# Hybrid attention and convolution layer: two transfers moved to ScalarE's queue, fewer warm-up matmuls, and a new order of work from changed planning constants

## Chip, cores and metric

The kernel runs on one core of a Trainium2 chip. The metric is the device time of one execution in microseconds (us); the median of several runs counts. A profile is one execution recorded by the hardware profiler.

## The reference, cut to what matters

```python
h = rmsnorm(x, norm_g)                      # x: 1024 x 1024 float32
proj = h @ w_in                             # w_in: 1024 x 5632
q, k, v, a_gate, c_val, c_glu, c_gate = split(proj)
# 16 query heads, 4 key/value heads of 64; softmax over three dilated causal windows
y_att = attention_branch(q, k, v, a_gate)   # (window, dilation): (128,1) (512,4) (2048,16)
# depthwise causal convolution of 31 taps over c_val * sigmoid(c_glu), layer norm, silu, gate
y_conv = conv_branch(c_val, c_glu, c_gate, ...)
x = x + concat(y_att, y_conv) @ w_out       # w_out: 2048 x 1024
out = rmsnorm(x, final_norm_g)
```

## The kernel before

All large products run on TensorE (PE) in a split form: a float32 operand is stored as a rounded high part and the remainder (hhi and hlo for the normalised input, wh and wl for the weights), and a product is three matmuls, high by high, low by high and high by low. ScalarE (ACT) makes the high part by a cast (line 250), VectorE (DVE) or a DMA that adds (line 298, on GpSimd's queue, POOL) the remainder.

The phases follow one another and overlap. In the **opening** (`prepare(0)`, lines 556 to 603) the eight blocks x0 to x7 of 128 rows are loaded, their mean squares taken (x0 by ACT, x1 by DVE, the others by ACT), the rows scaled by DVE (line 590) with the gain that PE has spread over the partitions (`gbc`, line 568), transposed by PE (`xT`), and split. Meanwhile PE runs `WARM` dummy transposes into a bank called `idle` (line 548), and `MORE` further ones after the first blocks (line 596). `parameters()` loads the taps and norm parameters into `rows` and has PE transpose them (`par_ps`, line 610). In the **body** PE computes 44 column blocks of the projection (`ps`), scores and outputs of 8 pairs of heads, while DVE convolves; which piece is issued in which section is in `SECTIONS`. In the **passage** to the end, the layer norm of the convolved channels (`layer_norm`, tiles cc, lst, rb) meets the first half of the product with w_out (`att_part`: ya is loaded, split into yha and yla, and multiplied by woah and woal into opsa). In the **last phase** (`conv_part`) yc is loaded and split for eight blocks of 128 rows, multiplied into opsc, added to z, normalised and stored.

No order of instructions is written by hand. Every operation goes into a list (`Plan.op`) with an engine and a cost. `Plan.order` (lines 304 to 421) simulates the engines with these costs and with limits on how many buffers of a group are live (`LIMITS`), and picks for each engine the operation that can start first, by priority among those that are ready. A priority is the position in the list less a boost; `TUNE` holds the boosts of the kinds of work. The order so found is fixed for each engine, SP (which issues most DMAs) and POOL included. So a constant of the simulated costs changes the order of all engines. A DMA is simulated here:

```python
if e in ("SP", "POOL"):
    dma = max(dma, t + 1.1) + self.dma_time[i]
    done = dma + 0.9
```

`dma_time` is the size by 300 GB/s for SP and by 175 GB/s otherwise. `after=` in `load` adds a dependency for the plan alone: `ya` is planned after the last woal (line 1034).

Of the kernel before, what the change touches and what calls it, by code (L numbers as in the profile page):

```python
# [16 lines left out]
P = 128  # L17
# [14 lines left out]

LIMITS = {"x": 5, "raw": 1, "raw_oc": 1, "raw_oa": 2, "wh": 3, "wl": 3, "tab": 2, "e": 7, "pt": 4, "vs": 4, "vc":
          4, "turn": 2, "opsa": 2, "score": 2, "hc": 5, "c": 7, "t": 1, "g": 1, "gl": 7, "y": 2, "ag": 4, "cc": 5,
          "qs": 5, "qf": 4, "kdh": 9, "kdl": 6, "yc": 2, "ya": 2, "zc": 7, "za": 3}

RESERVE = {"e": 7, "pt": 3}
BANKS = {"mm": 3, "sc": 2, "tp": 2, "o": 1}  # L40
WARM = 55
LATE = C_CG + 6 * P
MORE = (10, 12)
TUNE = {"w": 195, "use": 240, "ln": 65, "att": 240, "conv": 5, "wo": 215, "woa": -20, "ap": 0, "wait": 0.2116}
SECTIONS = [("k0 q0 h1 v", 0), ("h2 a0 q1", 1), ("h3 a1 q2 a2", 1), ("q3 h4", 1), ("h5 k1 a3 q4", 1), ("h6 a4 q5",
            1), ("c0 h7 a5 q6", 1), ("c1 q7 a6 a7 c2 c3", 1), ("c4 c5", 1), ("c6 c7", 0)]


def score_tables():
# [105 lines left out]
def ap_of(v):  # L155
    return v.ap() if isinstance(v, View) else v
# [5 lines left out]
class Plan:  # L162
# [5 lines left out]
    def __init__(self, tc, slots, limits):  # L168
        self.tc, self.nc = tc, tc.nc
        self.slots = slots  # L170
        self.limits = limits
        self.ops = []
        self.hold = []
        self.moved = []
        self.prio, self.boost = [], 0
        self.ranks = {}
        self.tables = {}
# [115 lines left out]
    def load(self, out, src, after=None):  # L293

        self.op("SP", 0.48, lambda: self.nc.sync.dma_start(out.ap(), ap_of(src)), [out], [src, after])

    def add_into(self, dst, x):
        self.op("POOL", 1.0, lambda: self.nc.gpsimd.dma_start(ap_of(dst), x.ap(), accum_op=ALU.add), [dst], [x, dst])  # L298

# [4 lines left out]
    def order(self):  # L304
        ops = self.ops
        n = len(ops)
        users, need = [[] for _ in ops], [0] * n
        for i, (_, _, _, deps, _) in enumerate(ops):
            need[i] = len(deps)
            for d in deps:  # L310
                users[d].append(i)
        left = {}
        for _, _, _, _, bufs in ops:
            for b in bufs:
                left[b] = b.left
        free = {k: [(0.0, j) for j in range(v[2])] for k, v in self.slots.items()}
        held, inuse, taken, bank = set(), {}, {}, {}
        clock = {e: 0.0 for e in ("PE", "ACT", "DVE", "SP", "POOL")}
        ready = {e: [] for e in clock}
        at = [0.0] * n  # L320
        self.when = at[:]
        for i in range(n):
            if not need[i]:
                ready[ops[i][0]].append(i)
        dma, table = 0.0, None
        out = []
        reserving = [i for i, op in enumerate(ops) if any(b.group in RESERVE for b in op[4])]
        first, last = reserving[0], reserving[-1]

        done_ops, oldest = [False] * n, 0  # L330

        def start_of(i):
            if i > oldest + self.ahead:
                return None
            t = max(at[i], clock[ops[i][0]])
            want, groups = {}, {}
            for b in ops[i][4]:
                if not b.fixed and b not in held:
                    want[b.kind] = want.get(b.kind, 0) + 1
                    if b.group:  # L340
                        groups.setdefault(b.group, []).append(b.rank)
            for k, c in groups.items():
                if inuse.get(k, 0) + len(c) > self.limits[k] or max(c) != taken.get(k, 0) + len(c) - 1:
                    return None
            for b in ops[i][4]:
                if b in bank and bank[b][0] != ops[i][0]:
                    t = max(t, bank[b][1])
            for k, c in want.items():
                keep = 0
                if k == "c4" and i > oldest + 16:  # L350
                    if first - self.near < oldest <= last and not any(g in RESERVE for g in groups):
                        keep = sum(max(n - inuse.get(g, 0), 0) for g, n in RESERVE.items())
                    if i > oldest + self.near:
                        keep += self.spare
                if len(free[k]) < c + keep:
                    return None
                t = max(t, sorted(free[k])[c - 1][0])
            return t

        while len(out) < n:  # L360
            best = None
            for e, todo in ready.items():
                now, pick = None, None
                for i in sorted(todo, key=self.prio.__getitem__):
                    t = start_of(i)
                    if t is None:
                        continue
                    soon = t - TUNE["wait"] if self.prio[i] < i - 300 else t
                    if now is None or soon < now - 1e-9:
                        now, pick, start = soon, i, t  # L370
                        if soon <= clock[e]:
                            break
                if pick is not None and (best is None or start < best[0]):
                    best = (start, pick)
            if best is None:
                raise RuntimeError(f"no slots: {oldest}, {inuse}, { {k: len(f) for k, f in free.items()} }, "
                                   f"{[(i, [b.name for b in ops[i][4]]) for r in ready.values() for i in sorted(r)[:3]]}")
            t, i = best
            e, cost, _, _, bufs = ops[i]
            if i in self.tables and self.tables[i] != table:  # L380
                table = self.tables[i]
                cost += 1.3
            ready[e].remove(i)
            for b in bufs:
                if not b.fixed and b not in held:
                    held.add(b)
                    if b.group:
                        inuse[b.group] = inuse.get(b.group, 0) + 1
                        taken[b.group] = taken.get(b.group, 0) + 1
                    b.slot = min(free[b.kind])[1]  # L390
                    free[b.kind].remove(min(free[b.kind]))
            end = t + cost
            clock[e] = end
            done = end + self.LATENCY
            if e in ("SP", "POOL"):
                dma = max(dma, t + 1.1) + self.dma_time[i]
                done = dma + 0.9
            elif e == "DVE":
                done = end + 0.13
            for b in bufs:  # L400
                if b.kind in PSUM_KINDS:
                    bank[b] = (e, done)
            same = {"PE": end, "ACT": end + 0.03}.get(e, done)
            for u in users[i]:
                at[u] = max(at[u], same if ops[u][0] == e else done)
                need[u] -= 1
                if not need[u]:
                    ready[ops[u][0]].append(u)
            for b in bufs:
                left[b] -= 1  # L410
                if not left[b] and not b.fixed:
                    free[b.kind].append((done, b.slot))
                    if b.group:
                        inuse[b.group] -= 1
            self.when[i] = t
            out.append(i)
            done_ops[i] = True
            while oldest < n and done_ops[oldest]:
                oldest += 1
        self.clock = clock  # L420
        return out

    def trace(self):
# [1 line left out]
        last = {}  # L425
        self.dma_time = {}
        for i, (e, _, _, _, bufs) in enumerate(self.ops):
            if e in ("SP", "POOL"):
                self.dma_time[i] = 4.0 * self.moved[i] / (300e3 if e == "SP" else 175e3)
        for i in self.order():  # L430
            engine, _, fn, _, bufs = self.ops[i]
# [32 lines left out]
def layer_kernel(tc, x, norm_g, w_in, conv_w, conv_b, ln_g, ln_b, w_out, fin_g, tab, out):  # L464
# [91 lines left out]
    def prepare(half):  # L556
        xs = []
        for j in range(4):
            tb = 4 * half + j
            xs.append(c4([P, D], f"x{tb}"))  # L560
            pl.load(xs[j], x[tb * P:(tb + 1) * P, :])
            if tb == 1:
                pl.load(gain, norm_g.rearrange("(o d) -> o d", o=1))
            if tb in first_w:
                raw[tb] = load_raw(first_w[tb])
# [494 lines left out]
    def conv_part(tb):  # L1060
# [18 lines left out]
        if final:  # L1079
            pl.tt(z[:, 0:512], z[:, 0:512], fin[:, 0:512], ALU.mult)  # L1080
            pl.act(z[:, 0:512], z[:, 0:512], AF.Copy, scale=r)
            pl.store(out[rows, 0:512], z[:, 0:512])
            pl.stt(z[:, 512:D], z[:, 512:D], r, fin[:, 512:D], ALU.mult, ALU.mult)
            pl.store(out[rows, 512:D], z[:, 512:D])
        else:
# [79 lines left out]
```

## Time and profile before

| what | us |
|---|---|
| median of three runs | 899.86 |
| lowest and highest run | 898.11, 900.07 |
| the profiled execution's own time | 898.14 |
| its span, first to last instruction | 896.3 |
| PE busy in the span | 873.2 |
| DVE busy | 655.8 |
| ACT busy | 592.8 |
| POOL busy | 53.3 |

The span is what the trace covers; the execution's own time has 1.8 us more around it. PE busy is the time with at least one matmul under way, dummies included. In the rows below, times are us from the start of the span; `<-` in brackets names what ended an idle time; SPq is SP's queue of DMA issues and PEld PE's loading of weights. PEclk is the granted TensorE clock as a share of full speed.

### The profile page before, as it was taken

What the parts mean: (1) busy time and instruction counts of PE and PEld (TensorE: products, weight loads), DVE (VectorE), ACT (ScalarE), POOL (GpSimd) and SP (SyncE); (2) the same over time, 40 slices, a digit from 0 to 9 for tenths busy, and PEclk for the clock granted to TensorE, in tenths of its full rate; (3) what the DMA queues carried; (4) which work ended last, traced back from release to release, by engine and by line L of the source; (5) the groups of instructions that cost most, each with busy time, mean ns of one, the idle gap of its engine ahead of it and who ended that gap; (6) DMA issues with size and microseconds to landing.
All of it is one profiled execution on the core that took longest, in us unless ns stands there. A gap on an engine that the chain in (4) does not pass through costs nothing.

```text
span 896.3 us, 13046 instructions
## 1 busy us (share of the span) xinstructions
PE 873.2 (97%) x4493; PEld 720.2 (80%) x4493; DVE 655.8 (73%) x1506; ACT 592.8 (66%) x1392; POOL 53.3 (6%) x69
## 2 busy tenths in 40 slices
PE   8999999999999999999999999999999799999996
PEld 7888888888888788887887887888787678878885
DVE  5769996689699689789989779943649895625333
ACT  4777368677958867977977947983896744414111
POOL 0001001010010010010010110101000000000000
PEclk9999999999999999999999999999999799999999
DMA  7533607254553474545355744455773697777111
GB/s 266 164 71 58 153 3 165 50 116 77 138 111 81 100 150 108 139 71 143 78 112 143 165 94 130 89 137 112 217 261 141 204 363 238 252 217 229 71 48 47
DMA packets 104953, 123.53 MB, mean 138 GB/s; under 512 B 17941, under 2 KB 78357, under 8 KB 104888
## 3 DMA queue, kind: packets, MB, share of 16 engines
q1 hardware_dynamic: 97000, 94.40, 34.3%
q0 software_dynamic: 7888, 28.32, 17.9%
q8 instruction: 35, 0.57, 0.3%
q14 instruction: 30, 0.25, 0.1%
HBM read 65.35 MB, written 24.84 MB: 101 GB/s over the span
## 4 chain that ended last, share of the span: by engine, by line
PE 86%; DMA 7%; DVE 3%; ACT 2%; issue 1%; SPq 1%; POOL 0%; DVEq 0%; ACTq 0%; POOLq 0%
PE ps L237 52%; PE opsc L237 10%; PE opsa L237 7%; PE sc_near L237 3%; PE on L237 3%; PE of L237 3%; PE sc_far L237 2%; DMA y<-comb 2%; PE tp_p L235 1%; PE tp_m L235 1%; DMA rows<-in_ln_b 1%; PE tp_s L235 1%; DMA raw_oc<-in_w_out 1%; ACT e L252 1%; DMA yc<-yc_dram 1%; DMA x<-in_x 1%
## 5 line engine op out<-in xcount | busy, mean ns | idle before, releaser
L237 PE MATMUL ps<-hhi,wh 128*128 128x512 f32 (+1 forms) x720 | 288.1, 401 | 0.3 <-ACT hhi L250 0.2
L237 PE MATMUL ps<-hlo,wh 128*128 128x512 f32 (+1 forms) x720 | 279.6, 390 | 0.3 <-DVE hlo L265 0.3
L237 PE MATMUL ps<-hhi,wl 128*128 128x512 f32 (+1 forms) x720 | 188.7, 395 | 0.0
L237 PEld LDWEIGHTS ps<-hhi,wh 128*128 128x128 f32 x720 | 135.6, 188 | 31.4 <-issue 0.5
L237 PEld LDWEIGHTS ps<-hlo,wh 128*128 128x128 f32 x720 | 135.8, 189 | 27.6 <-DVE hlo L265 0.8
L237 PEld LDWEIGHTS ps<-hhi,wl 128*128 128x128 f32 x720 | 129.3, 188 | 27.9
L252 ACT ACTIVATE e<-e,near 128x256 f32<-128x256 f32 (+1 forms) x256 | 115.6, 488 | 22.2 <-DVE near L265 12.3
L269 DVE SCALAR_TENSOR_TENSOR c<-hc,taps,c 128x511 f32<-128x511 f32 (+14 forms) x120 | 88.4, 737 | 0.3
L269 DVE SCALAR_TENSOR_TENSOR c<-t,taps,c 128x511 f32<-128x511 f32 (+14 forms) x120 | 88.6, 738 | 0.0
L269 DVE SCALAR_TENSOR_TENSOR t<-hc,taps,t 128x511 f32<-128x511 f32 (+6 forms) x112 | 82.5, 736 | 0.8 <-ACT t L252 0.8
L237 PE MATMUL opsc<-woc,yhc 128*128 128x512 f32 (+1 forms) x272 | 80.8, 381 | 0.0
L252 ACT ACTIVATE e<-e,far 128x224 f32<-128x224 f32 (+1 forms) x128 | 54.0, 424 | 36.0 <-DVE far L284 35.7
L298 POOL DMA_DIRECT2D wl<-raw x40 | 34.7, 868 | 452.1 <-ACT wl L252 350.1
L237 PEld LDWEIGHTS opsc<-woc,yhc 128*128 128x128 f32 x272 | 50.2, 188 | 10.6
L252 ACT ACTIVATE fjunk<-zc 128x512 bf16<-128x512 f32 (+1 forms) x17 | 10.3, 606 | 68.0 <-DVE zc L265 67.8
L237 PE MATMUL opsc<-woc,ylc 128*128 128x512 f32 (+1 forms) x136 | 52.0, 382 | 1.5 <-DVE ylc L265 1.5
L284 DVE CUSTOM_DVE_ANT_0 e<-sc_near,tab 128x256 f32<-128x256 f32 (+1 forms) x128 | 45.0, 404 | 9.9 <-PE sc_near L237 9.2
L250 ACT CAST wh<-raw 128x1024 fp32r<-128x1024 f32 x44 | 46.0, 1044 | 1.6 <-DMA raw<-in_w_in 1.4
L237 PE MATMUL opsa<-woah,yla 128*128 128x512 f32 x112 | 45.5, 406 | 1.5 <-DVE yla L265 1.5
L237 PE MATMUL opsa<-woah,yha 128*128 128x512 f32 x112 | 45.4, 405 | 0.0
L237 PE MATMUL opsa<-woal,yha 128*128 128x512 f32 x112 | 45.0, 402 | 0.0
L252 ACT ACTIVATE e<-e,f 128x96 f32<-128x96 f32 (+1 forms) x128 | 44.5, 439 | 0.2 <-DMA f<-back 0.2
(166 smaller groups left out, 1405.1 us busy)
## 6 DMA issues: line engine op xcount, KB each, us to landing
raw<-in_w_in SPq DMA_DIRECT2D x44, 512.0 KB, 4.5
wl<-raw POOLq DMA_DIRECT2D x40, 512.0 KB, 4.9
x<-in_x SPq DMA_DIRECT2D x8, 512.0 KB, 8.5
tab<-in_tab SPq DMA_DIRECT2D x8, 512.0 KB, 3.4
c_dram<-c SPq DMA_DIRECT2D x8, 512.0 KB, 3.3
g_dram<-g SPq DMA_DIRECT2D x8, 512.0 KB, 2.8
raw_oa<-in_w_out SPq DMA_DIRECT2D x8, 512.0 KB, 5.7
raw_oc<-in_w_out SPq DMA_DIRECT2D x8, 512.0 KB, 7.4
```

Of the source, the lines that this page charges most:

```text
L235: nc.tensor.transpose(out.ap(), a.ap(), b.ap())
L237: nc.tensor.matmul(out.ap(), a.ap(), b.ap(), start=start, stop=stop)
L250: nc.scalar.copy(out.ap(), x.ap())
L252: nc.scalar.activation(out.ap(), x.ap(), func, **{k: ap_of(v) for k, v in kw.items()})
L269: lambda: self.nc.vector.scalar_tensor_tensor(out.ap(), a.ap(), ap_of(s), b.ap(), op0, op1),
L284: lambda: self.nc.vector.tensor_tensor_reduce(out.ap(), a.ap(), b.ap(), 1.0, ap_of(first), ALU.add, ALU.min, least.ap()),
L298: self.op("POOL", 1.0, lambda: self.nc.gpsimd.dma_start(ap_of(dst), x.ap(), accum_op=ALU.add), [dst], [x, dst])
```

## The change

x1 is loaded by ACT's queue, and the first half of the last output block is stored by it. The dummies go from 55 to 26, those after the first two blocks from 10 and 12 to 8 and 8. The plan assumes that a DMA lands 1.9 us after its bytes have moved instead of 0.9, counts the two DMAs on ACT as DMAs (at the rate of those not on SP), and gets other limits, boosts and sections.

```diff
-LIMITS = {"x": 5, "raw": 1, "raw_oc": 1, "raw_oa": 2, "wh": 3, "wl": 3, "tab": 2, "e": 7, "pt": 4, "vs": 4, "vc":
-          4, "turn": 2, "opsa": 2, "score": 2, "hc": 5, "c": 7, "t": 1, "g": 1, "gl": 7, "y": 2, "ag": 4, "cc": 5,
-          "qs": 5, "qf": 4, "kdh": 9, "kdl": 6, "yc": 2, "ya": 2, "zc": 7, "za": 3}
+LIMITS = {"x": 5, "raw": 1, "raw_oc": 1, "raw_oa": 2, "wh": 4, "wl": 3, "tab": 1, "e": 7, "pt": 4, "vs": 4, "vc":
+          4, "turn": 2, "opsa": 2, "score": 2, "hc": 7, "c": 7, "t": 1, "g": 1, "gl": 7, "y": 2, "ag": 4, "cc": 4,
+          "qs": 6, "qf": 4, "kdh": 9, "kdl": 5, "yc": 1, "ya": 2, "zc": 8, "za": 3}
-WARM = 55
+WARM = 26
-MORE = (10, 12)
-TUNE = {"w": 195, "use": 240, "ln": 65, "att": 240, "conv": 5, "wo": 215, "woa": -20, "ap": 0, "wait": 0.2116}
-SECTIONS = [("k0 q0 h1 v", 0), ("h2 a0 q1", 1), ("h3 a1 q2 a2", 1), ("q3 h4", 1), ("h5 k1 a3 q4", 1), ("h6 a4 q5",
-            1), ("c0 h7 a5 q6", 1), ("c1 q7 a6 a7 c2 c3", 1), ("c4 c5", 1), ("c6 c7", 0)]
+MORE = (8, 8)
+TUNE = {"w": 215, "use": 120, "ln": 65, "att": 240, "conv": -105, "wo": 155, "woa": -240, "ap": 20, "wait": 0.2116}
+SECTIONS = [("k0 q0 h1 v", 0), ("h2 a0 q1", 1), ("h3 a1 q2", 1), ("a2 q3 h4", 1), ("h5 k1 a3 q4", 1), ("h6 a4 q5",
+            1), ("c0 h7 a5 q6", 1), ("a6 c1 a7 q7 c2", 1), ("c5 c4 c3", 1), ("c6 c7", 0)]
...
+        self.sent = set()
...
+    def load_act(self, out, src):
+        self.op("ACT", 0.1, lambda: self.nc.scalar.dma_start(out.ap(), ap_of(src)), [out], [src])
+        self.sent.add(len(self.ops) - 1)
+
+    def store_act(self, dst, x):
+        self.op("ACT", 0.1, lambda: self.nc.scalar.dma_start(ap_of(dst), x.ap()), [dst], [x])
+        self.sent.add(len(self.ops) - 1)
...
-            if e in ("SP", "POOL"):
+            if e in ("SP", "POOL") or i in self.sent:
                 dma = max(dma, t + 1.1) + self.dma_time[i]
-                done = dma + 0.9
+                done = dma + 1.9
...
-            same = {"PE": end, "ACT": end + 0.03}.get(e, done)
+            same = done if i in self.sent else {"PE": end, "ACT": end + 0.03}.get(e, done)
...
-            if e in ("SP", "POOL"):
+            if e in ("SP", "POOL") or i in self.sent:
                 self.dma_time[i] = 4.0 * self.moved[i] / (300e3 if e == "SP" else 175e3)
...
-            pl.load(xs[j], x[tb * P:(tb + 1) * P, :])
+            (pl.load_act if tb == 1 else pl.load)(xs[j], x[tb * P:(tb + 1) * P, :])
...
-            pl.store(out[rows, 0:512], z[:, 0:512])
+            pl.store_act(out[rows, 0:512], z[:, 0:512])
```

## Rows read from the trace of the kernel before

**Rows 1.** Windows: stretch, length, PE, PEld, DVE, ACT, POOL busy (instructions), PEclk, DMA share, GB/s.
```profile
0.00:25.00 25.00, 20.71 (x142) 18.24 (x142) 13.82 (x30) 12.93 (x23) 1.02 (x8) 0.95 0.78 260
...
675.00:704.00 29.00, 22.86 (x99) 16.87 (x97) 26.82 (x43) 20.44 (x29) 0.00 (x0) 0.91 0.58 195
...
850.00:897.00 47.00, 38.92 (x191) 32.37 (x190) 14.15 (x35) 7.62 (x23) 0.00 (x0) 0.96 0.12 49
sum 897.00, PE 873.23 PEld 720.16 DVE 655.78 ACT 592.75 POOL 53.26; mean PE 45.96 PEld 37.90 DVE 34.51 ACT 31.20 POOL 2.80
```

**Rows 2.** Windows of PE alone in the passage: length, PE busy, PEclk, DMA share, GB/s.
```profile
700.00:705.00 5.00, 3.60 (x12) 0.50 1.08 347
705.00:710.00 5.00, 5.00 (x16) 0.63 0.67 211
```

**Rows 3.** Timeline of the opening: start, us, engine, line, operation, [idle before <-releaser].
```profile
0.74 1.28 ACT L252 ACT_TABLE_LOAD   x1 [0.74 <-PEq L1157]
0.74 0.87 SPq L295 DMA_DIRECT2D x<-in_x  x2
...
1.45 8.23 PE L235 MATMUL idle<-ident 128*128 128x128 f32 x55 [1.45 <-POOL ident masks.py:199]
...
4.49 1.06 ACT L252 ACTIVATE junk<-x 128x1024 bf16<-128x1024 f32 x1 [2.25 <-DMA x<-in_x]
...
5.81 1.23 DVE L290 CUSTOM_DVE_ANT_0 junk<-x 128x1024 bf16<-128x1024 f32 x1 [3.96 <-DMA x<-in_x]
...
9.61 1.98 PE L237 MATMUL gbc<-gain,avg 1*128 1x512 f32 x4
...
10.77 2.92 DVE L269 SCALAR_TENSOR_TENSOR x<-x,xst,gbc 128x512 f32<-128x512 f32 x4 [2.42 <-PE gbc L237]
...
21.54 0.66 PE L235 MATMUL par_ps<-ident,rows 34*128 34x34 f32 x8 [1.70 <-DMA rows<-in_ln_b]
```

**Rows 4.** PE's groups, 0 to 6 us, then 6 to 9 us: busy us, mean ns.
```profile
L235 PE MATMUL idle<-ident 128*128 128x128 f32 x23 | 4.7, 398 | 1.5 <-POOL ident masks.py:199 1.5
L235 PE MATMUL idle<-ident 128*128 128x128 f32 x30 | 3.4, 272 | 0.0
```

**Rows 5.** Windows of PE alone in the opening, the row from 3 to 4 us.
```profile
3.00:4.00 1.00, 1.00 (x6) 1.00 0.94 373
```

**Rows 6.** The tail: SP's timeline, then the stores of the tensor `out_dram`.
```profile
892.30 0.81 SPq L301 DMA_DIRECT2D out_dram<-zc  x2
...
L301 SPq DMA_DIRECT2D out_dram<-zc x9: 332/333/383, 815.9 to 892.7; - x9
```

**Rows 7.** DMA issues of the whole kernel: count, KB each, median us to landing.
```profile
raw<-in_w_in SPq DMA_DIRECT2D x44, 512.0 KB, 4.5
...
tab<-in_tab SPq DMA_DIRECT2D x8, 512.0 KB, 3.4
...
raw_oc<-in_w_out SPq DMA_DIRECT2D x8, 512.0 KB, 7.4
...
ya<-y_dram SPq DMA_DIRECT2D x8, 448.0 KB, 7.9
```

**Rows 8.** Timelines in the passage (SP, PE, ACT), and the tile woal.
```profile
696.07 0.39 SPq L295 DMA_DIRECT2D ya<-y_dram  x1
...
700.48 2.05 PE L237 MATMUL rb<-ident,lst 128*128 128x128 f32 x8 [4.28 <-DVE lst L269]
...
701.00 0.94 ACT L250 CAST yha<-ya 128x896 fp32r<-128x896 f32 x1 [0.22 <-DMA ya<-y_dram]
...
L265 DVE TENSOR_TENSOR woal<-raw_oa,woah x8: 1209/1216/1221, 643.5 to 696.3; 128x1024 fp32r<-128x1024 f32 x8
```

**Rows 9.** Last phase: the chain that ended last, and the tile yc.
```profile
799.90 89.04 PE opsc L237 x406
...
L250 ACT CAST yhc<-yc x8: 1032/1050/1054, 796.5 to 826.2; 128x1024 fp32r<-128x1024 f32 x8
L265 DVE TENSOR_TENSOR ylc<-yc,yhc x8: 1214/1219/1226, 798.6 to 829.2; 128x1024 fp32r<-128x1024 f32 x8
...
DMA to landing us min/median/max: 5.9/7.1/10.8
```

## The prediction

> **What bounds the kernel now.** I read the table of busy time by stretch first. PE is busy 873.23 us of a span of 896.3, so the bound is PE's own work plus 23.1 us in which it stands [rows 1]. Those stand in three places. In the first 25 us PE is idle 4.3 us; in the last row it is idle 8.1 us, of which 0.7 lie beyond the span, so 7.4 us; what is left, 23.1 - 4.3 - 7.4 = 11.4 us, is in the body. Of this, 6.1 us stand in one stretch, 675 to 704 us [rows 1], where the last projections end and the products with w_out begin. The reader is to see there also a granted clock of 0.91. The finer rows give its price: PE is busy 3.60 us at clock 0.50, then 5.00 us at 0.63 [rows 2]. At half level, 3.60 us does 1.8 us of work. A mean of 0.63 over 5 us is 3.7 us at the lower level (1.2 GHz) and 1.3 at the upper (2.4 GHz), which loses another 1.85. So this passage costs 6.1 + 1.8 + 1.9 = 9.8 us. Elsewhere the stalls are short, and DVE, ACT and DMA matter only through them. Thus there are three places to look at: the opening, the passage, and the tail after the last matmul.
>
> **Opening: fewer dummies.** The timeline of the opening shows PE on 55 dummies from 1.45 to 9.68, then the gain broadcast (gbc) at 9.61. DVE, which has the statistics of x0 and x1 finished earlier, stands 2.42 us until gbc comes, and normalises at 10.77 [rows 3]. With 26 dummies: 23 of them start before 6.0 us, and the later ones are faster, at a mean of 272 ns (pipelined) against 398 [rows 4]. The remaining 32 start in the 3.6 us to 9.6, 0.11 us each, so the 26th starts near 6.3 and PE is free at about 6.5. gbc then comes 3.1 us sooner, at 6.5; its first bank served DVE 1.16 us after its start (10.77 - 9.61), so would at 7.7. DVE's idle time began at 10.77 - 2.42 = 8.35, hence gbc is no longer last and the whole 2.42 us come off this step.
>
> What is late next? PE's transposes of the parameters (par_ps) wait 1.70 us for a landing of `rows<-in_ln_b` and start at 21.54 [rows 3]. PE takes its instructions in order. If par_ps keeps its place ahead of the transposes of x2, PE merely waits there 2.4 us longer and nothing is gained. If the new plan puts it behind them, the 2.4 us stay. The plan now assumes all loads 1.0 us later, both x2 and the parameter rows, so neither order is favoured. I take half, -1.2. Ends: -2.4, and +1.25 if less PE activity keeps the clock low for as long again as now (granted 0.95 over 25 us withholds 1.25 us of full-speed time [rows 1]). The cuts of MORE from 10 and 12 to 8 and 8 remove six fast dummies, 0.7 us that fit in PE's wait for DVE; I cost them at nothing. If that cover is gone they are worth 0.7, inside these ends.
>
> **Opening: x1 by ACT.** SP issues x0 and x1 in 0.87 us [rows 3], so gain, raw and x2 are issued about 0.43 us sooner. ACT issues x1 at 0.74 instead of some 1.18, if the issue stands before its table load. Behind the load of 1.28 us it would go out at 2.02, 0.84 us later [rows 3]. Behind this instruction on ACT stand only the table load and the warm-up; ACT then stands until x0 lands at 4.49, so they delay nobody. Would x1 land sooner? x0 is there at 4.49, x1 at 5.81, 1.32 us apart. From 3 to 4 us the 16 DMA engines are already at a share of 0.94 and move 373 GB/s [rows 5]: no room is left for a second stream. The Trainium skill (DMA: Bandwidth & Descriptors, Issuing engines are not separate DMA queues) says that transfers issued by the scalar, sync or gpsimd engine run on the same 16 DMA engines and interleave, so that a second issuer saves only issue time; the row agrees. By a queue with bandwidth of its own, x1 would land with x0 and the sum would be 1.3 us lower; by the rule, it stays. Interleaved, x0 may come as late as 5.81; ACT's 1.06 us over it then end about with DVE's 1.23 us over x1, so nothing is lost. I take 0; ends -1.3 and +0.8.
>
> **Tail.** Two stores of the last block go out on SP, together 0.81 us from 892.30 [rows 6]; the second starts at 892.7. Both halves are computed by then, so with ACT issuing the first, SP's comes 0.4 us sooner. I take -0.4. No ACT issue is in this trace; ends 0.4 better and 0.4 worse, the size of the one issue.
>
> **The replanned body.** This is the largest and least certain term. The order of every engine is recomputed from the constants in the diff. For a 512 KB load the old plan counts 1.1 us to start, 1.75 us at 300 GB/s and 0.9 us to land, 3.75 us. The new one counts 4.75. The trace has 4.5 for raw, 7.4 for raw_oc, 7.9 for ya [rows 7]. So for the weights of the body the new assumption is about right, and there the old order showed no long stall anyway. For the passage it closes 1.0 of a shortfall of 7.4 - 3.75 = 3.65 us, that is 27%. The passage shows how a late load works: ya is issued on SP at 696.07, its cast yha starts at 701.00, and PE, after 4.28 us of waiting for the layer norm's rb, has no product to fill that gap with [rows 8]. In 27% of 9.8 us I see 2.65; I take -2.5. Ends: -9.8 (the passage closes) and +4.9 (below). The moved pieces in SECTIONS, the other TUNE and LIMITS numbers remove and add no matmul; they act through this term alone.
>
> One limit needs a line of its own: yc falls from 2 buffers to 1. A block of the last phase takes PE 89.04 / 8 = 11.1 us. One buffer's turn is 7.1 us to land, 1.05 us of cast and 1.22 us of subtraction, 9.4 us [rows 9]. PE's work on the previous block hides it with 1.7 us to spare; I cost it at 0. A load of 10.8 us, the slowest seen, would take 13.1 us, 2.0 more than the block: the upper end is +2.0, once. The single tab buffer is covered too: its load takes 3.4 us and is made eight times in the whole kernel, once per pair of heads [rows 7].
>
> **Sum:** -1.2 + 0 - 0.4 - 2.5 + 0 = -4.1 us. The profiled execution took 898.14 us, 1.8 outside its span; it becomes 894.0. The median of the three runs, 899.86, lies 1.7 higher; on its level I predict 895.8. A difference under 0.2%, 1.8 us, can hardly be told from none here.
>
> **Rivals.**
> 1. *The gain meets the next gate.* par_ps keeps its place and the passage its length: only the tail's 0.4 us is left, 899.5. For it speaks that the wait before par_ps ends with a DMA and not with PE's work; against it, that the plan's assumption of landing changes by 1 us everywhere. Chance 0.22.
> 2. *Slower: the attention weights of w_out come later.* TUNE's woa goes from -20 to -240, the lowest priority of all. The eight woal subtractions are 1.216 us each on DVE, the last starting at 696.3 [rows 8], and the load of ya is planned behind them. If four more of the eight fall into the passage, ya and PE's first product are 4 x 1.216 = 4.9 us later. That gives 899.86 - 0.4 + 4.9 = 904.4. From 2.2 us later on, with the tail alone gained, it is slower by over 0.2%. Against it: DVE is planned with its true load, and lower priority only counts where work is ready to go first. Chance 0.22.
> 3. *The passage closes.* With weights, ya and layer norm ordered by later landings, PE finds projections to fill it: -9.8 - 0.4 - 1.2, or 888.5. Against it: 4.75 us is still far from 7.4 and 7.9. Chance 0.16.
> 4. The forecast itself, 893 to 898: chance 0.40.
>
> Faster is 0.40 + 0.16 = 0.56, the same 0.22, slower 0.22. The range from 888 to 903 leaves out about 2 in 10, half of rival 2 and the far side of rival 3.
>
> **What would show it.** DVE's normalisation of x0 near 8.4 us, not 10.77, with no wait for gbc; then whether par_ps still stops PE at about 21.5 or stands behind transposes of x2. x1's statistics starting within 0.5 us of 5.8. The last store issued 0.4 us sooner after the last DVE instruction. In the stretch around 675 to 710, PE's idle time near 4.5 us instead of 6.1 and less time at the low clock. PE's total idle time near 19 us. The prediction is wrong if that passage keeps or lengthens its idle time, if the body gains new stalls of several us, or if PE is at the low clock when the first product starts.

## The result and the profile after

The changed kernel takes 885.22 us (median of 4 runs, 884.62 to 887.45) against 899.38 before (4 runs, 898.11 to 900.07): a ratio of 0.985, with a 95% interval from 0.983 to 0.987. Its profiled execution took 884.98 us, its span is 883.0, 13.3 shorter. Forecast were 895.8 us and 888 to 903: the sign was right, the size was not, and the time lies below the range.

The table of busy time of the changed kernel by stretch answers to [rows 1]; its columns are the same, and code lines are one higher than before.

```profile
0.00:25.00 25.00, 18.32 (x99) 15.48 (x100) 14.31 (x29) 13.14 (x23) 1.03 (x8) 0.88 0.83 270
675.00:704.00 29.00, 26.57 (x114) 21.13 (x113) 25.79 (x43) 21.64 (x33) 0.00 (x0) 0.94 0.63 203
704.00:750.00 46.00, 46.00 (x209) 37.74 (x208) 32.82 (x55) 19.71 (x29) 0.00 (x0) 1.00 0.89 313
850.00:897.00 47.00, 26.00 (x136) 21.95 (x134) 10.18 (x26) 5.25 (x16) 0.00 (x0) 0.94 0.09 34
```

PE's idle time in the opening grew from 4.3 to 6.7 us (25 - 18.32) and the mean clock fell from 0.95 to 0.88: the opening is worse, not better. In the passage the idle time fell from 6.1 to 2.4 us. In the last row PE is idle 21.0 us, 14.0 of them beyond the span, so 7.0 against 7.4 before.

Where the 13.3 us came from is best read at two marks that both kernels pass with the same products behind them: the last projection (tile ps, 3 x 720 matmuls) and the first product of the last phase (tile opsc). First the rows of the two tiles in the kernel before, then in the changed one; behind the durations stand the first and the last start.

```profile
L237 PE MATMUL ps<-hhi,wl x720: 277/394/505, 18.7 to 692.7; 128*128 128x512 f32 x172, 128*128 128x256 f32 x8
L237 PE MATMUL opsc<-woc,yhc x272: 277/393/402, 797.8 to 888.5; 128*128 128x512 f32 x120, 128*128 128x256 f32 x16
```

```profile
L238 PE MATMUL ps<-hhi,wl x720: 277/394/562, 23.8 to 687.1; 128*128 128x512 f32 x172, 128*128 128x256 f32 x8
L238 PE MATMUL opsc<-woc,yhc x272: 276/393/404, 784.9 to 875.6; 128*128 128x512 f32 x120, 128*128 128x256 f32 x16
```

Opening and body end 5.6 us sooner (687.1 against 692.7). The passage from there to opsc takes 97.8 us instead of 105.1, 7.3 less. The rest of the span is 98.1 instead of 98.5, 0.4 less. Together 13.3. Within the first part I counted, for each matmul that isn't a dummy, the median spacing of its kind in the trace before: by 45 us PE had lost 17.3 us before and 18.0 after. So the opening costs 0.7 us more, and the body gives 6.3.

These are the rows of one execution of each kernel, and this execution of the kernel before was one of its faster ones (898.14 us; the medians of the kernel before beside the experiments are 900.2 to 902.9). old_joined (below), which gives every engine the same order up to the passage, passes its last projection at 696.6 us, not 692.7. So the share of the body is known to some 4 us only.

**The body.** PE's windows there, of the kernel before and of the changed one (length, PE busy, clock, DMA share, GB/s):

```profile
300.00:330.00 30.00, 27.91 (x168) 1.00 0.49 115
```

```profile
300.00:330.00 30.00, 30.00 (x174) 1.00 0.61 129
```

A stall of 2.1 us between 309.9 and 314.6 us, in three pieces, where PE waited for ACT's exponentials and DVE's pt (the same exponentials transposed and split), is gone. By the count of spacings, 3.5 of the 6.3 us lie between 300 and 330 us. Only 2.9 of the 6.3 were recorded as idle before. A 128x512 projection is recorded with 394 ns (the rows above), while the next starts 233 ns after it, both medians. So a wait of less than some 160 ns leaves no gap; that the rest of the 6.3 is such waits is inferred from this, not seen.

**The passage.** The timeline of the changed kernel, to be held against [rows 8]:

```profile
685.11 0.98 SPq L296 DMA_DIRECT2D ya<-y_dram  x2
...
687.29 0.95 PE L238 MATMUL var<-avg,ss 128*128 128x1 f32 x8
...
691.49 1.09 DVE L266 TENSOR_TENSOR yla<-ya,yha 128x896 fp32r<-128x896 f32 x1
...
691.58 2.05 PE L238 MATMUL rb<-ident,lst 128*128 128x128 f32 x8 [2.37 <-DVE lst L270]
...
693.27 0.77 PE L238 MATMUL opsa<-woah,yha 128*128 128x512 f32 x1
```

The kernel before, in the same columns as the changed one's third row above, and then the reciprocal in the chain to lst (the layer norm's factor of each row, which PE spreads as rb) on DVE, before and after:

```profile
704.00:750.00 46.00, 45.08 (x184) 35.85 (x185) 37.04 (x58) 25.34 (x38) 0.00 (x0) 0.95 0.81 281
```

```profile
698.64 0.17 DVE L280 RECIPROCAL lst<-lst 128x4 f32<-128x4 f32 x1
```

```profile
690.66 0.18 DVE L281 RECIPROCAL lst<-lst 128x4 f32<-128x4 f32 x1 [0.43 <-ACT lst L253]
```

The loads of ya go out 2 us before the last projection starts its last matmul, not 3.4 us after it as before (696.07 against 692.7). yla, subtracted at 691.49, is there when opsa begins. PE waits once, 2.37 us for lst instead of 4.28, and its clock is low from 691.5 to 694.9 us instead of for the 10.2 us from 698.5. The wait for lst is shorter because DVE is free for it: before, DVE did a woal and two woc subtractions first and took the reciprocal 1.4 us after ACT's square root had ended (697.22), now it stands 0.43 us waiting for that square root.

**Opening and tail.** The changed kernel's timeline, which answers to [rows 3] and [rows 6]:

```profile
0.74 0.39 SPq L296 DMA_DIRECT2D x<-in_x  x1
...
1.44 0.44 ACTq L300 DMA_DIRECT2D x<-in_x  x1
...
1.46 6.71 PE L236 MATMUL idle<-ident 128*128 128x128 f32 x42 [1.46 <-POOL ident masks.py:199]
...
5.88 1.23 DVE L291 CUSTOM_DVE_ANT_0 junk<-x 128x1024 bf16<-128x1024 f32 x1 [4.02 <-DMA x<-in_x]
...
8.09 1.98 PE L238 MATMUL gbc<-gain,avg 1*128 1x512 f32 x4
...
9.56 2.06 DVE L270 SCALAR_TENSOR_TENSOR x<-x,xst,gbc 128x512 f32<-128x512 f32 x3
...
19.39 1.04 PE L236 MATMUL par_ps<-ident,rows 34*128 34x34 f32 x8 [3.87 <-DMA rows<-in_ln_b]
...
879.05 0.38 ACTq L304 DMA_DIRECT2D out_dram<-zc  x1
879.08 0.33 SPq L311 DMA_DIRECT2D out_dram<-zc  x1
```

All 42 dummies, MORE's included, stand ahead of gbc. PE begins the first product earlier (13.01 us, 16.13 before) and then stands 3.87 us at par_ps until the parameter rows land. The two last stores go out at the same time. Still the end of the span comes 3.92 us after the last store's issue instead of 3.62, so little of the 0.4 us is gained.

### The profile page after: what moved, and what is told of

It reads as the page before. It is cut to its first block, busy times and chain, and to the rows that moved or that the text cites. A ratio compares the mean times of both kernels' runs of the same rounds, so it can differ in the third digit from the quotient of the medians.

```text
span 883.0 us, 12948 instructions
## 1 busy us (share of the span) xinstructions
PE 865.5 (98%) x4458; PEld 717.0 (81%) x4458; DVE 656.2 (74%) x1506; ACT 591.2 (67%) x1392; POOL 53.3 (6%) x69
## 4 chain that ended last, share of the span: by engine, by line
PE 96%; DMA 2%; DVE 0%; ACT 0%; issue 0%; SPq 0%; ACTq 0%
PE ps L238 57%; PE opsa L238 10%; PE opsc L238 10%; PE sc_near L238 3%; PE on L238 3%; PE sc_far L238 3%; PE of L238 3%; PE tp_m L236 2%; PE tp_p L236 2%; PE tp_s L236 1%; DMA rows<-in_ln_b 1%; PE tp_w L236 1%; DMA x<-in_x 1%; PE xT L236 1%; PE y L238 0%; PE rb L238 0%
## 5 line engine op out<-in xcount | busy, mean ns | idle before, releaser
L238 PE MATMUL ps<-hhi,wl 128*128 128x512 f32 (+1 forms) x720 | 192.6, 398 | 0.0
L253 ACT ACTIVATE e<-e,near 128x256 f32<-128x256 f32 (+1 forms) x256 | 115.5, 490 | 22.7 <-DVE near L285 17.3
L285 DVE CUSTOM_DVE_ANT_0 e<-sc_far,tab 128x224 f32<-128x224 f32 (+1 forms) x128 | 35.8, 319 | 12.6 <-PE sc_far L238 12.4
```

The source lines that it names most:

```text
L238: nc.tensor.matmul(out.ap(), a.ap(), b.ap(), start=start, stop=stop)
L253: nc.scalar.activation(out.ap(), x.ap(), func, **{k: ap_of(v) for k, v in kw.items()})
L285: lambda: self.nc.vector.tensor_tensor_reduce(out.ap(), a.ap(), b.ap(), 1.0, ap_of(first), ALU.add, ALU.min, least.ap()),
```

## The experiments

At first two theories. **A, landing:** the later landing in the plan's simulation makes the better order. **B, numbers:** LIMITS, TUNE and SECTIONS do. The rival **C** was that any new order scatters the time by so much, and that only the whole set was fitted to itself. Ratios are to the kernel before, run with them on the same chip. Here the marks of the profiled executions together, one of each kernel (that of new_land09 took 890.07 us, 3.4 over its median; from tile rows and spans; "passage" is from the last start of ps to the first of opsc). All kernels have the same matmuls, dummies left out, behind them at both marks:

| kernel | median us | ratio (95%) | last ps at | passage | rest |
|---|---|---|---|---|---|
| before | 899.38 | 1 | 692.7 | 105.1 | 98.5 |
| changed | 885.22 | 0.985 (0.983, 0.987) | 687.1 | 97.8 | 98.1 |
| old_land19 | 903.78 | 1.002 (0.999, 1.004) | 691.3 | 112.5 | 98.2 |
| new_land09 | 886.67 | 0.984 (0.980, 0.988) | 694.0 | 96.3 | 98.0 |
| old_numbers_new | 887.46 | 0.984 (0.981, 0.988) | 690.4 | 95.9 | 98.1 |
| new_numbers_old | 906.24 | 1.005 (1.002, 1.008) | 694.4 | 112.5 | 98.2 |
| old_sections_new | 892.68 | 0.990 (0.987, 0.994) | 692.6 | 99.7 | 98.6 |
| old_tune_new | 904.86 | 1.003 (1.001, 1.005) | 701.7 | 103.6 | 98.4 |
| old_limits_new | 903.23 | 1.002 (0.999, 1.005) | 698.8 | 105.3 | 98.0 |
| old_sections_tune | 905.19 | 1.004 (1.002, 1.007) | 697.1 | 106.3 | 98.1 |
| old_sections_limits | 903.08 | 1.002 (1.000, 1.005) | 703.3 | 100.2 | 98.2 |
| old_tune_limits | 904.79 | 1.003 (1.000, 1.006) | 701.6 | 103.5 | 98.3 |
| old_joined | 899.47 | 0.998 (0.996, 1.000) | 696.6 | 104.1 | 98.2 |
| new_woa_old | 884.57 | 0.980 (0.976, 0.983) | 686.6 | 98.7 | 98.0 |
| changed_again | 884.81 | 0.982 (0.978, 0.985) | 686.9 | 97.9 | 98.1 |
| frozen_par_late | 882.50 | 0.978 (0.975, 0.982) | 684.9 | 97.6 | 98.0 |
| frozen_warm55 | 883.41 | 0.981 (0.977, 0.984) | 685.5 | 96.9 | 98.0 |
| frozen_sp | 885.40 | 0.983 (0.980, 0.986) | 687.6 | 97.9 | 98.1 |
| frozen_both | 883.94 | 0.979 (0.977, 0.982) | 686.9 | 97.6 | 98.0 |

The last column is the first thing to see: the last phase takes 98.0 to 98.6 us in every order. Nearly all that the kernels differ by lies before it.

### Landing or numbers

old_land19 is the kernel before with the later landing alone; new_land09 undoes it in the changed kernel.

```diff
-                done = dma + 0.9
+                done = dma + 1.9
```

> The kernel before with the landing of 1.9 us as its only edit. Theory A (the assumed landing removes the stalls): the passage between projections and output product loses about 5 us instead of 11, PE is idle about 15 us in all instead of 23, time 890 to 894. Theory B (the new limits, boosts and sections remove them): passage and time as before, 897 to 902. Theory C (every replan scatters and only the pair was fitted to each other): a time off by 3 us or more to either side, with stalls in other places than before.

> The changed kernel with the landing put back to 0.9 us. Theory A: the passage loses about 11 us again and some stalls in the body return, 893 to 899. Theory B: the same as the changed kernel, 884 to 888. Theory C: 888 to 900, with stalls that neither kernel has.

old_numbers_new is the kernel before with the new LIMITS, TUNE and SECTIONS and nothing else (55 dummies, SP's transfers, landing 0.9); new_numbers_old is the reverse, the changed kernel with the three old ones.

```diff
-LIMITS = {"x": 5, "raw": 1, "raw_oc": 1, "raw_oa": 2, "wh": 3, "wl": 3, "tab": 2, "e": 7, "pt": 4, "vs": 4, "vc":
+LIMITS = {"x": 5, "raw": 1, "raw_oc": 1, "raw_oa": 2, "wh": 4, "wl": 3, "tab": 1, "e": 7, "pt": 4, "vs": 4, "vc":
...
-TUNE = {"w": 195, "use": 240, "ln": 65, "att": 240, "conv": 5, "wo": 215, "woa": -20, "ap": 0, "wait": 0.2116}
+TUNE = {"w": 215, "use": 120, "ln": 65, "att": 240, "conv": -105, "wo": 155, "woa": -240, "ap": 20, "wait": 0.2116}
...
```

> The kernel before with only the limits, boosts and sections of the changed one (landing 0.9 us, 55 dummies, all transfers as before). Theory A: no gain, 896 to 902. Theory B: the gain of passage and body, 885 to 889. Theory C: between or beyond, up to 905.

> The changed kernel with the limits, boosts and sections of the one before (landing 1.9 us, 26 dummies, both transfers on ACT's queue). Theory A: the gain stays, 885 to 892. Theory B: only the tail's 0.4 us is left, 897 to 901. Theory C: as of the first run, scattered by 3 us or more.

The numbers alone give 0.984, as much as the whole change; all the rest without them gives 1.005. The landing assumption makes no difference that these runs can tell, in either kernel. Theory A falls. Theory C fails for these edits: three different plans made with the new blocks (changed, new_land09, old_numbers_new) come out at 0.984 or 0.985 beside the kernel before, and no kernel without all three blocks is below 0.990. For parts of the blocks it comes back below. What the later landing does to the passage by itself is in the waits and the PE windows of old_land19:

```profile
PE opsa L237 <- DVE yla L265: 8.8, 2, 7.6
PE rb L237 <- DVE lst L269: 3.8, 2, 2.1
```

```profile
735.00:740.00 5.00, 1.99 (x11) 0.79 1.04 409
740.00:745.00 5.00, 0.00 (x0) 0.50 0.24 100
```

The first wait for rb is halved, as the prediction hoped, and a later block of opsa then stands 7.6 us for its yla: the passage is 7.4 us longer than in the profile before. new_numbers_old, with the same landing and the same old numbers, has the same wait (8.4 us in two) and the same 112.5.

### Which of the numbers

Each of the three blocks alone in the kernel before, then each pair; the edits are the lines above and this one:

```diff
-SECTIONS = [("k0 q0 h1 v", 0), ("h2 a0 q1", 1), ("h3 a1 q2 a2", 1), ("q3 h4", 1), ("h5 k1 a3 q4", 1), ("h6 a4 q5",
+SECTIONS = [("k0 q0 h1 v", 0), ("h2 a0 q1", 1), ("h3 a1 q2", 1), ("a2 q3 h4", 1), ("h5 k1 a3 q4", 1), ("h6 a4 q5",
...
```

> The kernel before with only the new SECTIONS (a2 one section later, another order of the last pieces). Theory S (the sections remove the stalls of the body, above all the 2.6 us of PE waits near 310 us): those waits gone, the passage as before, 894 to 898 on the level of 899.4. Theory W (all the gain is in the passage and comes from the boosts): no gain, within 2 us of the kernel before. Theory C (only the set together helps, since each number moves the whole order): a time off by 3 us or more, either sign.

> The kernel before with only the new TUNE (convolution and attention weights of w_out at low priority). Theory S: the passage shrinks by up to 7 us and the waits near 310 us stay, 891 to 895 on the level of 899.4. Theory W: all of the gain, 884 to 889. Theory C: off by 3 us or more, either sign, and not the gain of the whole set.

> The kernel before with only the new LIMITS. Theories S and W: no gain, 897 to 902 on the level of 899.4. Theory C: off by 3 us or more, either sign.

> The kernel before with the new SECTIONS and TUNE, old LIMITS. Theory P (the order of pieces and the low priorities of convolution and w_out weights work together in the passage): nearly the whole gain, a ratio to the kernel before near 0.985 to 0.987, passage at 2 to 4 us lost. Rival theory L (limits are needed with the sections): a ratio near 0.990 as with the sections alone, passage at about 6 us lost, or worse as with TUNE alone.

> The kernel before with the new SECTIONS and LIMITS, old TUNE. If sections and limits carry the gain and the boosts only add to it: a ratio of 0.984 to 0.988. If the three have to be fitted to each other: near 0.990, as the sections alone, or worse, up to 1.005.

> The kernel before with the new TUNE and LIMITS and the old SECTIONS. So far against the kernel before: SECTIONS alone 0.990, TUNE alone 1.003, LIMITS alone 1.002, SECTIONS with TUNE 1.004, SECTIONS with LIMITS 1.002, all three 0.984. Theory P (TUNE and LIMITS belong together as a pair, and SECTIONS adds its own 1%): the pair alone is worth 0.984 / 0.990 = 0.994, some 894 to 897 us, and the wait of PE for rb in the passage is near 2.4 us while the stall at 310 to 316 us remains. Theory S (the pieces' places in SECTIONS are the ground of the gain, and the other two only refine an order that SECTIONS has changed): without SECTIONS the pair gives nothing, 1.000 to 1.006, and a stall of several us stands in the body or the passage. Theory O (the three numbers fit only as a set, found together, and any part of them gives an order of its own without relation to the whole): anything from 0.990 to 1.006, with stalls at places where neither the kernel before nor the changed one has them.

SECTIONS alone is worth 1%, TUNE and LIMITS alone nothing or a little worse. No pair keeps the 1%, and all three together give 1.6%. What the single steps would add up to has no relation to the whole. Waits of PE in one execution of each pair, of old_sections_tune (in the passage, and near 460 us), of old_sections_limits and of old_tune_limits (near, far and comb are tiles of the attention that DVE works on):

```profile
PE opsa L237 <- DVE yla L265: 7.0, 2, 5.7
PE sc_far L237 <- DVE far L284: 4.1, 5, 1.4
```

```profile
PE of L237 <- DVE comb L265: 3.0, 1, 3.0
...
PE ps L237 <- DMA wl<-raw: 2.4, 1, 2.4
PE opsa L237 <- DVE yla L265: 2.1, 1, 2.1
```

```profile
PE sc_near L237 <- DVE far L284: 4.7, 2, 4.4
PE rb L237 <- DVE lst L269: 4.0, 1, 4.0
```

In old_sections_limits the passage is mostly cured (100.2 us) and the last projection starts 10.6 us later than in the profile before (6.7 later than in old_joined), with waits for comb and wl that neither the kernel before nor the changed one shows. In old_tune_limits the long wait for rb is there as before. Its wait of 4.4 us at 633 us can't be put down to the pair: old_joined, in the order of the kernel before, has it too with 3.4 us, and old_tune_new with 3.1. So the idea that TUNE and LIMITS are a pair with a gain of its own falls too. That the three fit as a set, and parts of it don't, is shown by the medians, and to that extent theory C was right; which rule of the plan's simulation makes them fit was not found.

new_woa_old, the changed kernel with TUNE's woa at -20 again, asks about the second rival of the prediction.

```diff
-TUNE = {"w": 215, "use": 120, "ln": 65, "att": 240, "conv": -105, "wo": 155, "woa": -240, "ap": 20, "wait": 0.2116}
+TUNE = {"w": 215, "use": 120, "ln": 65, "att": 240, "conv": -105, "wo": 155, "woa": -20, "ap": 20, "wait": 0.2116}
```

> The changed kernel with the one boost woa put back from -240 to -20. If the low priority of the attention weights of w_out makes the passage short: 3 us or more over the changed kernel, 888 to 893. If it is a nudge among many: within 2 us of it, 883 to 887.

884.57 us: this priority neither gains nor costs anything that can be measured.

### The passage by hand

**Theory J:** seven operations at the first join of layer norm and opsa make the passage long. old_joined keeps the order of the kernel before and moves only these up: the first load of ya ahead of the last store of g, the chain to lst and the cast yha right behind ACT's square root, and yla behind the next two subtractions of woc.

```diff
+        put([3609], 3593)
+        put([3674, 3675, 3676, 3677, 3610], 3673, True)
+        put([3611], 3670, True)
```

> The kernel before in the order of its own plan with seven operations of the passage moved up: the first load of ya ahead of the last store of g, the layer norm's reciprocal chain and the cast yha right behind the square root on ACT, yla behind the next two weight subtractions. Theory J (the passage's loss is the place of these few): rb starts near 698 us instead of 700.5, the first product runs without the wait for yla, the low clock is shorter, the passage loses 5 to 8 us instead of 11.4, the time 3 to 6 us under the kernel before. Rival theory (the passage waits for loads or DVE's total work whatever the order): the wait moves to another instruction there, within 1.5 us of the kernel before.

Its waits of PE:

```profile
PE sc_near L237 <- DVE far L284: 3.6, 2, 3.4
PE rb L237 <- DVE lst L269: 2.2, 1, 2.2
PE opsa L237 <- DVE cc L265: 2.1, 1, 2.1
```

The wait for rb falls from 4.28 to 2.2 us, and 2.1 us come back at a later opsa, which waits for cc. The passage is 1.0 us shorter, not 7.3; the median 899.47 against 901.24, with an interval that ends at 1.000. Theory J said 3 to 6 us and a lost 5 to 8 in the passage; this is nearer to its rival, in which the wait moves to another instruction. The join is at most a small part of the passage's loss: here a later block needed its operands sooner too.

### The opening

**Theory G (gate):** the first product's earlier start is lost at par_ps, and PE's standing there costs clock. frozen_par_late keeps every engine's order of the changed kernel and only holds par_ps and what depends on it back until x3 is transposed. All frozen kernels keep that order: the simulation gets the changed kernel's inputs.

```diff
+            if gate is not None and (i in late or self.ops[i][3] & late):
+                late.add(i)
+                wait.append(i)
+                continue
```

> The changed kernel in the very order that its plan gives, except that PE's transposes of the parameters, and what needs them, come after the transposes of x3 instead of inside the first product. Theory G (the gain of the opening is lost at that gate): the wait of 3.9 us for the parameter rows is gone, PE is not at the low clock near 20 us, all later work comes 1.5 to 3.5 us sooner, 882 to 884. Rival theory (x2, x3 and the second weight tile are late anyway): the wait moves to the transposes of x2, and the time stays within 1 us of the changed kernel, 884 to 886.

The opening of frozen_par_late, to be held against the changed kernel's first row above:

```profile
0.00:25.00 25.00, 20.47 (x119) 16.61 (x120) 14.72 (x30) 12.65 (x22) 1.03 (x8) 1.00 0.82 268
```

and finer, of the changed kernel (PE alone):

```profile
16.00:18.00 2.00, 0.00 (x0) 1.00 1.00 375
...
20.00:22.00 2.00, 2.00 (x12) 0.50 0.81 218
```

Without the gate no wait for the rows is left, the clock stays at 1.00, and 882.50 us is the lowest median of all the kernels here. The changed kernel did not run on that chip, and the ratios (0.978 here, 0.982 and 0.985 for the changed kernel) have intervals that overlap or nearly meet, so the gain rests on the trace: the span is 2.5 us shorter than the changed kernel's, nearly all of it before the last projection (684.9 against 687.1).

frozen_warm55 has the changed kernel's order with 29 more dummies at the front, 71 in one run; frozen_both has the 29 and the late par_ps.

```diff
-    pl.mm([(idle[:, 0:P], ident, ident, None, None)] * WARM)
+    pl.dummies((idle[:, 0:P], ident, ident, None, None), WARM, 55)
```

> The changed kernel in the very order of its plan, with 29 more dummies run at its start (55 as before, instead of 26). Theory G (the start of the first product does not matter, since PE waits for the parameter rows behind it): the gain broadcast and the first product come 3 us later, the wait of 3.9 us for the parameter rows shrinks by as much, the time is within 1 us of the changed kernel, or up to 2 us under it if the dummies keep the clock up. Rival theory (the dummies are on the path): about 3 us over the changed kernel.

> The changed kernel in the order of its plan, with the parameter transposes after those of x3 and with 29 more dummies at its start. If gate and clock are one loss, already paid back by either: 882 to 884, as with one of them. If the later start now shows, since nothing gates PE behind it: 2 to 3 us over the kernel with the gate moved alone, 884 to 886. If they add up: 880 to 881.5.

changed_again is the changed kernel unedited, beside them on the same chip.

> The changed kernel itself, unedited, beside the next three on one chip: about 1.5% under the kernel before, 884 to 888. It is the level for the two frozen orders of this set.

The half of theory G on the clock doesn't hold in changed_again. There the granted clock falls within the window from 12 to 14 us, before PE stands at par_ps:

```profile
12.00:14.00 2.00, 1.32 (x5) 0.53 0.79 221
```

```profile
19.05 1.03 PE L236 MATMUL par_ps<-ident,rows 34*128 34x34 f32 x8 [2.09 <-DMA rows<-in_ln_b]
```

The first product starts at 13.52 us at the lower level. Its slower matmuls fill part of the time in which PE would wait for the rows, so the wait is 2.09 us instead of 3.87, and by 45 us PE has lost 17.8 us, no more than the changed kernel's 18.0.

The timeline of frozen_warm55:

```profile
1.45 10.16 PE L314 MATMUL idle<-ident 128*128 128x128 f32 x71 [1.45 <-POOL ident masks.py:199]
11.54 1.98 PE L238 MATMUL gbc<-gain,avg 1*128 1x512 f32 x4
...
20.64 0.65 PE L236 MATMUL par_ps<-ident,rows 34*128 34x34 f32 x8 [1.77 <-DMA rows<-in_ln_b]
```

It starts the products (16.35) 3.3 us later than the changed kernel and 2.8 later than changed_again, waits 1.8 us at par_ps instead of 3.9 and 2.1, loses no clock, and takes 883.41 against 884.81 of changed_again: with the gate in place, the fewer dummies seem to cost some 1.4 us (five of changed_again's six runs lie above all six of frozen_warm55, the sixth, 880.88, below them all). With the gate moved the sign may turn, which is not shown: frozen_both, 2.6 us later at the first product (16.52 against 13.91), takes 883.94 against 882.50 (on another chip, so by the ratios 0.979 and 0.978 the two can't be told apart; the profiled spans are 882.5 and 880.5).

frozen_sp sends x1, right behind x0, and the half store by SP again.

```diff
-        self.op("ACT", 0.1, lambda: self.nc.scalar.dma_start(out.ap(), ap_of(src)), [out], [src])
+        self.op("ACT", 0.1, lambda: self.nc.sync.dma_start(out.ap(), ap_of(src)), [out], [src])
...
```

> The changed kernel in the very order of its plan, with x1 and the half output block issued by SP again. Theory G: the tail is 0.4 us longer, the opening is as long (x1 comes by the same bandwidth and the parameter rows gate PE anyway), the time 0 to 1 us over the changed kernel. Rival theory (a second queue carries data earlier): the opening too is longer, 1.5 to 3 us over it.

885.40 against 884.81 on the same chip, with overlapping runs. In its trace the last stores go out at 879.62 and 880.05, 0.43 us apart where the changed kernel issues them together, yet its rest of the span is 98.1 us as there, and x1's statistics start at 5.97 us instead of 5.88.

## Why the prediction was right or wrong

**The replanned body** is the step that failed. "The moved pieces in SECTIONS, the other TUNE and LIMITS numbers remove and add no matmul; they act through this term alone": the term was then sized by the landing assumption, as 27% of the passage's 9.8 us, and -2.5 was taken. The runs show the opposite split. The landing assumption gives nothing (1.002 alone, and 0.984 without it); the three blocks of numbers give the whole gain. An order is changed by any of these constants, not only by the one that mends a cost. In place of -2.5 the trace has -7.3 in the passage and -6.3 in the body, 13.6 us.

**"The passage closes"**, the third rival, came near in size: -7.3 of the 9.8 that it allowed. But it is operands that are ready when PE comes to them, not projections that fill the wait, and the later landing had no part in it. That the time fell below even its 888.5 is due to the body. "Elsewhere the stalls are short" was true, but they were then left out of the sum: the lower end, -9.8, held only the passage, while 5.3 of the 11.4 us of idle time that the first paragraph counts lie outside the stretch that it prices, and waits too short to leave a gap don't show in idle time at all.

**Opening, fewer dummies:** -1.2 was taken, +0.7 was measured, inside the end of +1.25. Two steps failed. MORE's cut was to cost nothing since these dummies fit in PE's wait for DVE; the new order puts all of them ahead of gbc, which came at 8.09 instead of 6.5. And DVE's normalisation began at 9.56, not 8.4, since ACT made a cast of weights (7.52 to 8.56) before the square root that it needs; that it would no longer wait for gbc was right. The question "what is late next?" was the right one: par_ps kept its place, the first rival's mechanism, and its wait grew by 2.2 us where 2.4 was said, which is partly luck, since it grew by 0.4 in changed_again. With the place changed (frozen_par_late) the opening is worth 0.7 - 2.2 = -1.5 us by the last projection's start, near the -1.2. The end that reckoned with less activity and a lower clock is what happened: 0.88 against 0.95. One of its signs of being wrong, the low clock at the first product, is absent from the first profile and present in changed_again.

**x1 by ACT:** 0 was taken. DVE begins with x1 at 5.88 us, before 5.81. The issue stood neither ahead of the table load nor wholly behind it: it went out at 1.44. The Trainium skill (DMA: Bandwidth & Descriptors, Issuing engines are not separate DMA queues) says that a second issuing engine brings no bandwidth of its own; the trace agrees, by 5.88 here and 5.97 in frozen_sp.

**Tail:** -0.4 was taken, and the two profiles differ by 0.4, but by luck. The last store does go out 0.4 us sooner; the span then ends 3.92 us after it instead of 3.62. frozen_sp, with both stores on SP, has the same rest, 98.1, as the changed kernel, and eight of the other nine kernels with both stores on SP have a shorter rest than this execution of the kernel before. So some 0.1 us is gained, and the term was too large.

**yc with one buffer:** 0 was taken. PE's wait for ylc is 1.4 us, before 1.5, once, and the last phase keeps its 98 us.

**The slower rival** (woal late) didn't happen: no wait for it is in the trace, and new_woa_old is as fast.

## What to carry to other kernels

When a change alters constants of a planner, don't size it by the one constant whose meaning you understand: compare the two orders at a few marks that both pass with the same work done, and price every stretch where the bounding engine stands, the short ones too. Constants that set one order together must be tested together: here one of three alone gave 1%, every pair nothing, the set 1.6%. And an earlier start is worth only what the next in-order wait leaves of it; look for an instruction in that queue whose operand is late, and move it.

## What the runs showed of the hardware

**One order, different times.** Beside the first experiments the kernel before ran from 894.66 to 906.75 us, 1.3%, in 19 executions. One place where this can arise: old_joined has the order of the kernel before up to the passage, and its PE waits 3.37 us for DVE before sc_near at 634 us, where the profiled execution of before waited 0.39. The changed kernel's ten runs, in two sets, lie between 880.88 and 887.45.

**The clock in the opening also differs between executions of one kernel.** changed_again has a mean of 0.74 over the first 25 us, the changed kernel 0.88, with the same instructions:

```profile
0.00:25.00 25.00, 20.07 (x101) 0.74 0.83 272
```

In frozen_warm55, after 71 dummies in a row, it reads 1.00 to 25 us and beyond; so it does in frozen_par_late with 42, so the number of dummies alone doesn't decide it.

The dummies are transposes. In the kernel before the first 23 start some 0.2 us apart and the later 32 some 0.11 (4.5 us / 23, 3.6 us / 32, with means of 398 and 272 ns [rows 4]). PE has done nothing but transposes by then, and the granted clock reads full while the faster ones run:

```profile
6.00:7.00 1.00, 1.00 (x11) 1.00 1.09 327
```

It reads 1.00 over the slower ones too [rows 5], so that these ran at the lower level is inferred from the halved spacing. The Trainium skill (TensorE: Matmul & The Clock Gate, Part 4: PE-mode transpose) says that the full clock doesn't engage for transposes; the trace differs, and the measurement decides.

**A small load can be late.** The last parameter row, 4 KB, is issued at 8.79 us and reaches PE at 19.39; the chain that ended last in the changed kernel names its stretch:

```profile
8.79 10.32 DMA rows<-in_ln_b
```

Ten microseconds for 4 KB, while raw with 512 KB takes a median of 4.1 from issue to landing. Want of room on all 16 engines isn't the whole reason: in the kernel before, the same load is under way from 9.87 to 21.29 us, and between 16 and 18 us its windows show a DMA share of 0.08 (the last but one column). In that time SP stands in the issue of one block of x, from 12.43 to 17.86 us.

```profile
16.00:18.00 2.00, 1.53 (x10) 1.00 0.08 28
```

What holds it was not tried. This load, not PE or DVE, sets when par_ps can run.
